# Side products of neighbouring heads and column tiles issued side by side, in a hybrid Mamba and attention layer pair

## The chip, the cores and the metric

The kernel runs on one core of one Trainium2 chip. The metric is the device time of one execution in microseconds (us); three runs of the kernel before gave 1612.24, 1612.61 and 1613.0 us, so the median is 1612.61 us. Every duration below comes from one profiled execution of the same kernel. Engines are called as the profile calls them: PE is the matrix engine, PEld its weight loads, DVE the vector engine, ACT the scalar engine, POOL the general-purpose engine, SP the engine whose queue issues most transfers.

## The reference

Two layers work on 256 tokens of width 2048, in 32-bit floats. The first is a Mamba2 layer with 64 heads in 8 groups, the second an attention layer with 32 heads of 128 channels whose logits carry a forget term. Cut to what the kernel has to compute:

```python
def mamba2_mixer(h, w_in, conv_w, conv_b, dt_bias, a_log, d_skip, norm_w, w_out):
    proj = h @ w_in                                  # 2048 -> 10304: z, x, B, C, dt
    xbc = silu(causal_depthwise_conv(xbc, conv_w, conv_b))
    y = ssd_chunked(xs, dt, a, bm, cm)               # (C B^T * decay) x, per head
    y = y + xs * d_skip
    y = gated_group_rmsnorm(y, z, norm_w)
    return y @ w_out                                 # 4096 -> 2048

def forgetting_attention_mixer(h, w_in, b_forget, w_out):
    proj = h @ w_in                                  # 2048 -> 16416: q, k, v, z, f
    cum = cumsum(log_sigmoid(f_logit + b_forget))
    for i in range(2):                               # blocks of 128 queries
        logits = q[i] @ k[:i + 1].T * scale + cum_q - cum_k, masked
        o[i] = softmax(logits) @ v[:i + 1]
    return (o * silu(z)) @ w_out                     # 4096 -> 2048

for i in range(2):
    x = x + mixer_i(rmsnorm(x, norm_w[i]))
return rmsnorm(x, final_norm_w)
```

The block of queries 0 to 127 sees only its own 128 keys, the block of queries 128 to 255 sees 256. Of each head's logits that makes a first block of 128x128 and a second of 128x256.

## The kernel before, in words

**Weight products.** Nearly all the work of PE is products of x or of an intermediate with weights that are streamed once from memory in tiles of 128x1024. A product of 32-bit floats is made of three products of a faster, shorter type (fp32r): ACT rounds a weight tile to its high form `wh` (`act_hi`, L102), DVE subtracts it from the tile and rounds the rest to the low form `wl` (`dve_lo`, L108), and the activations have high and low forms too. There are 7 buffers for raw tiles, 5 for `wh` and 4 for `wl`. Some of the products are arranged as Strassen-like sums, in which a tile is added to earlier ones as it is loaded (`sum_a`, `sum_b`, `sum_c`) and x is used in seven block combinations (`form`, `split_form`, L232).

**Side work.** Between the weight products stand small products and transposes that belong to no weight. In a Mamba group these are C times B transposed (`pcb`, L517), the transposes of the four 128-column tiles of x (`pxa`, L551), the product of the decay matrices with x for the head pair of each column tile (`py`, L598), the product with the state (`pof`) and the transposes of the gated result (`pyt`, L653). In a head of attention they are the transposes of q and k (`pqk`, L1017), the logits (`psc`, L1033), the transposes of the probabilities (`ppt`, L1069) and, at every second head, of z (`pz`, L1074), and the product with v (`po`, L1092 to L1095).

**What sets the order.** The program is a list of parts, each with the weight products of a half tile or of one sum. After each part `emit_due` issues the side work that has come due. `later(n, fn)` makes a step due n ordinary parts later; a part of a sum counts for half of one. For a head of attention the steps stand one part apart (`turn_qk`, `split_qk`, `logits`, `softmax`, `invert`, `turn`, `keep`, `values`, `close`), and the next head begins `gap` parts after the one before: 9 for most groups of four heads, 6 for the first and the last but one, 2 for the last. From this program a scheduler makes one fixed order of instructions for each engine, and PE, ACT, DVE, POOL and SP then run their own orders and wait for each other at semaphores.

**Accumulation banks.** In the Mamba layer 4 banks of PSUM hold weight products and 4 the side products, in the attention layer 5 and 3. A side step takes the next free bank of its pool.

**The layer boundary.** `to_layer2` (L780 to L788) adds the last output products to x, turns x (`pxt`, L795), rounds each of 16 tiles to a high and low form (`x`, L102 and L110), and makes the seven combinations of four pairs of tiles (`form`, then `ghx` on ACT and `glx` on DVE), which the first sums of the attention layer use. `stats2`, the forget gate (`forget`, `forget_sums`) and a round trip of its sums through memory (`cum_d`, `cB`) follow; each head's mask term `dd` (L1040) needs them.

Of the kernel before, what the change touches and what calls it, by code (L numbers as in the profile page):

```python
# [17 lines left out]
P = 128  # L18
# [5 lines left out]
G = 8  # L24
# [40 lines left out]
def hybrid_kernel(ctx: ExitStack, tc: tile.TileContext, a):  # L65
# [40 lines left out]
    def dve_lo(out, in_, hi, scale=None):  # L106
        if scale is None:
            nc.vector.tensor_tensor(out, in_, hi.bitcast(F32), op=ALU.subtract)  # L108
        else:
            nc.vector.scalar_tensor_tensor(  # L110
                out, in_, scale, hi.bitcast(F32), op0=ALU.mult, op1=ALU.subtract
            )

# [380 lines left out]
    def group_units(g):  # L494
# [13 lines left out]
        def post_c(ps):  # L508
            def done(o):
                st["C"] = o  # L510
                later(2, cb_pe)
                later(3, cb_dve)
            conv_silu(ps, 6 * g + 1, f"CT{g}", done)

        def cb_pe():
            st["pcb"] = pcb = bank(psa, "pcb")
            nc.tensor.matmul(pcb[:, 0:256], st["B"][:, 0:P], st["C"], start=True, stop=True)  # L517
            nc.tensor.matmul(pcb[:, 256:384], st["B"][:, P:S], st["C"][:, P:S],
                             start=True, stop=True)

        def cb_dve():
            st["cb"] = cb = lp.tile([P, 384], F32, tag="cb", name=f"cb{g}", bufs=2)
            nc.vector.tensor_tensor(cb, st["pcb"][:, :384], cst[:, C_MQ:C_MQ + 384],
                                    op=ALU.mult)
# [13 lines left out]
        def x_done(i, o):  # L538
            st[f"x{i}"] = o
            later(1 + wait, lambda: xa_pe(i))  # L540
            later(2 + wait, lambda: xa_dve(i))
            later(2 + wait + more, lambda: decay(i))
            later(4 + wait + more, lambda: y_pe(i))
            if i == 3:
                later(4 + wait + more, off_pe)
                later(5 + wait + more, off_dve)

        def xa_pe(i):
            st["pxa"] = pt = bank(psa, "pxa")
            for t in range(T2):  # L550
                nc.tensor.transpose(pt[:, t * P:t * P + P], st[f"x{i}"][:, t * P:t * P + P],  # L551
                                    ident)

        def xa_dve(i):
# [6 lines left out]
            c = slice(i * P, i * P + P)  # L561
            pt = st["pxa"]
            pt4 = pt[:, :S].rearrange("p (t h d) -> p t h d", t=T2, h=2)
# [10 lines left out]
        def decay(i):  # L574
            ee = lp.tile([P, 2, T2, P], F32, tag="ee", name="ee", bufs=3)
            for j in range(2):
                h = H0 + 2 * i + j
                for t in range(T2):
                    nc.scalar.activation(ee[:, j, t, :], st["acs"][i][:, j, t * P:t * P + P],
                                         AF.Relu, scale=-1.0, bias=beta[:, t, h:h + 1])  # L580
            nc.scalar.activation(ee, ee, AF.Exp, scale=-1.0)

            def mul():
                cb = st["cb"].rearrange("p (b l) -> p b l", b=3)
                nc.vector.tensor_tensor(
                    ee, ee, cb[:, 0:3:2, :].unsqueeze(1).to_broadcast([P, 2, T2, P]), op=ALU.mult)
                st[f"m{i}"] = ee
            later(1, mul)

# [24 lines left out]
        def post_z(pss, tiles):  # L614
# [12 lines left out]
            for i2 in range(2):  # L627
                later(4 + i2 + wait + more, lambda i2=i2: out_pe(i2))
                later(5 + i2 + wait + more, lambda i2=i2: out_split(i2))

# [144 lines left out]
    def to_layer2(n, t):  # L775


        if t == 1:
# [5 lines left out]
            if n == 3:  # L784
                later(2, stats2)
                for q in range(KS // 2):
                    later(2 + q, lambda q=q: split_form(
                        lay2["f"][q], True, lay2["forms"], 0, f"x{q}"))  # L788

    def x2_tiles(k0):  # L790
# [12 lines left out]
        for i in range(2):  # L803
# [7 lines left out]
            act_hi(xk[:, 0], pt[:, i * S:i * S + S], w)  # L811
            dve_lo(xk[:, 1], pt[:, i * S:i * S + S], xk[:, 0], w)

# [161 lines left out]
    def four_heads(hq, first=()):  # L975

        st = {}
        gap = {0: 6, G - 2: 6, G - 1: 2}.get(hq, 9)

# [3 lines left out]
        def vz_done(c):  # L983
# [9 lines left out]
            later(1, gate)  # L993
            steps = (turn_qk, split_qk, logits, softmax, invert, turn, keep, values, close)
            for i in range(4):
                for n, f in enumerate(steps, 1):
                    later(n + i * gap, lambda i=i, f=f: f(i))
# [23 lines left out]
        def split_qk(i):  # L1021
            h = fp[0].tile([P, 512], F32R, tag="qkh", name=f"qkh{hq}_{i}")
            l = fp[0].tile([P, 512], F32R, tag="qkl", name=f"qkl{hq}_{i}")
            act_hi(h, st["pqk"])
            dve_lo(l, st["pqk"], h)
            st["qkhl"] = (h, l)

        def logits(i):
            qkh, qkl = st["qkhl"]
            st["ps"] = ps = bank(psa, "psc")  # L1030
            for t, c, n in BLOCKS:
                for j, (q, k) in enumerate(((qkl, qkh), (qkh, qkh), (qkh, qkl))):
                    nc.tensor.matmul(ps[:, c:c + n], q[:, t * P:t * P + P], k[:, S:S + n],  # L1033
                                     start=j == 0, stop=j == 2)
            h = 4 * hq + i
# [251 lines left out]
```

## Time and profile before

| | |
|---|---|
| median of three runs | 1612.61 us (1612.24 to 1613.0) |
| the profiled execution, own time | 1618.07 us |
| its span | 1616.3 us |
| mean granted PE clock | 0.997 |
| PE busy | 1591.6 us, 98% of the span, 7862 instructions |
| DVE busy | 1342.0 us, 83% |
| ACT busy | 1061.6 us, 66% |
| POOL busy | 163.8 us, 10% |
| transfers | 362.30 MB, 224 GB/s over the span |

The profiled execution is 5.46 us longer than the median run, and 1.77 us of its time lies outside the span. The span is cut from one recorded execution; a row of a timeline gives the start, the duration, the engine, the line, the result and its inputs with the tile's shape, and how many instructions of that kind follow each other (x4). In brackets stands how long the engine idled before it and who released it. Starts of successive rows on PE tell the pace, since matmuls overlap and the duration of one row reaches into the next.

### The profile page before, as it was taken

What the parts mean: (1) busy time and instruction counts of PE and PEld (TensorE: products, weight loads), DVE (VectorE), ACT (ScalarE), POOL (GpSimd) and SP (SyncE); (2) the same over time, 40 slices, a digit from 0 to 9 for tenths busy, and PEclk for the clock granted to TensorE, in tenths of its full rate; (3) what the DMA queues carried; (4) which work ended last, traced back from release to release, by engine and by line L of the source; (5) the groups of instructions that cost most, each with busy time, mean ns of one, the idle gap of its engine ahead of it and who ended that gap; (6) DMA issues with size and microseconds to landing.
All of it is one profiled execution on the core that took longest, in us unless ns stands there. A gap on an engine that the chain in (4) does not pass through costs nothing. (4 is left out here: it accounts for less than half of the span.)

```text
span 1616.3 us, 22668 instructions
## 1 busy us (share of the span) xinstructions
PE 1591.6 (98%) x7862; PEld 1333.1 (82%) x7862; DVE 1342.0 (83%) x2006; ACT 1061.6 (66%) x1594; POOL 163.8 (10%) x214
## 2 busy tenths in 40 slices
PE   8999999999999999999999999999999999999997
PEld 6888888888888888778888888888888888888886
DVE  6888989798979897887888887888888887887886
ACT  7677777676767665755666665666665666676663
POOL 0000111011101110011100110010100101001000
PEclk9999999999999999999999999999999999999999
DMA  9665789778977897578887887897886987888843
GB/s 352 213 202 191 199 251 230 251 193 251 235 253 189 249 227 229 170 180 240 255 244 243 209 233 230 235 244 209 220 252 194 251 243 188 239 244 241 229 159 101
DMA packets 100964, 362.30 MB, mean 224 GB/s; under 512 B 11601, under 2 KB 12241, under 8 KB 100849
## 3 DMA queue, kind: packets, MB, share of 16 engines
q1 hardware_dynamic: 75888, 271.61, 48.4%
q0 software_dynamic: 24960, 89.24, 29.3%
q8 instruction: 62, 1.02, 0.2%
q14 instruction: 54, 0.43, 0.1%
HBM read 358.60 MB, written 2.20 MB: 223 GB/s over the span
## 5 line engine op out<-in xcount | busy, mean ns | idle before, releaser
L102 ACT ACTIVATE wh<-raw 128x1024 fp32r<-128x1024 f32 (+1 forms) x373 | 393.2, 1056 | 228.5 <-PE psa L288 73.8
L108 DVE TENSOR_TENSOR wl<-raw,wh 128x1024 fp32r<-128x1024 f32 (+1 forms) x373 | 451.5, 1216 | 82.4 <-issue 37.2
L102 ACT ACTIVATE wh<-sum_a 128x1024 fp32r<-128x1024 f32 x176 | 185.9, 1058 | 138.2 <-PE psy L924 32.6
L108 DVE TENSOR_TENSOR wl<-sum_a,wh 128x1024 fp32r<-128x1024 f32 x176 | 214.4, 1221 | 67.1 <-PE psu L924 36.6
L209 PE MATMUL pst<-x,wh 128*128 128x512 f32 x736 | 189.9, 398 | 0.1
L209 PEld LDWEIGHTS pst<-x,wh 128*128 128x128 f32 x736 | 134.0, 189 | 25.8 <-issue 0.5
L288 PE MATMUL psa<-wh,x 128*128 128x512 f32 x512 | 132.1, 399 | 0.0
L102 ACT ACTIVATE wh<-sum_b 128x1024 fp32r<-128x1024 f32 x88 | 93.2, 1060 | 55.1 <-PE psx L913 35.3
L108 DVE TENSOR_TENSOR wl<-sum_b,wh 128x1024 fp32r<-128x1024 f32 x88 | 106.7, 1219 | 9.8 <-issue 5.0
L288 PEld LDWEIGHTS psa<-wh,x 128*128 128x128 f32 x512 | 94.5, 188 | 21.6 <-issue 3.3
L213 PEld LDWEIGHTS pst<-x,wl 128*128 128x128 f32 x736 | 101.1, 192 | 7.5
L213 PE MATMUL pst<-x,wl 128*128 128x256 f32 x736 | 103.4, 284 | 0.0
L924 PE MATMUL psz<-wh,x 128*128 128x512 f32 x256 | 101.0, 394 | 0.0
L157 POOL DMA_DIRECT2D sum_a<-in_wf_s x64 | 55.3, 864 | 449.6 <-DVE wl L108 332.5
L924 PE MATMUL psv<-wh,x 128*128 128x512 f32 x256 | 100.6, 393 | 0.0
L924 PE MATMUL psy<-wh,x 128*128 128x512 f32 x256 | 99.8, 390 | 0.0
L924 PE MATMUL psu<-wh,x 128*128 128x512 f32 x256 | 99.7, 390 | 0.0
L690 DVE TENSOR_TENSOR xs<-psa,xs 128x512 f32<-128x512 f32 (+1 forms) x81 | 51.8, 678 | 26.1 <-PE psa L288 26.1
L288 PE MATMUL psa<-wh,ghf 128*128 128x512 f32 (+1 forms) x260 | 71.3, 394 | 0.0
L288 PE MATMUL psa<-wl,x 128*128 128x512 f32 x256 | 69.4, 391 | 1.2 <-DVE wl L108 1.2
L288 PE MATMUL psa<-wl,ghf 128*128 128x512 f32 (+1 forms) x260 | 69.4, 387 | 0.0
L288 PE MATMUL psa<-wh,glf 128*128 128x512 f32 (+1 forms) x260 | 69.3, 386 | 0.0
(356 smaller groups left out, 3312.7 us busy)
## 6 DMA issues: line engine op xcount, KB each, us to landing
raw<-in_wf_p SPq DMA_DIRECT2D x128, 512.0 KB, 4.9
raw<-in_wm_t SPq DMA_DIRECT2D x90, 512.0 KB, 4.8
raw<-in_wm_z SPq DMA_DIRECT2D x64, 512.0 KB, 5.4
sum_a<-in_wf_s POOLq DMA_DIRECT2D x64, 512.0 KB, 7.8
raw<-in_wf_o SPq DMA_DIRECT2D x64, 512.0 KB, 4.8
sum_a<-in_wm_s POOLq DMA_DIRECT2D x36, 512.0 KB, 5.9
sum_a<-in_wf_s SPq DMA_DIRECT2D x32, 512.0 KB, 6.8
sum_c<-in_wf_s SPq DMA_DIRECT2D x32, 512.0 KB, 5.3
```

What stands on the lines that cost most here:

```text
L102: nc.scalar.activation(out, in_, AF.Copy)
L108: nc.vector.tensor_tensor(out, in_, hi.bitcast(F32), op=ALU.subtract)
L157: nc.gpsimd.dma_start(u["sums"][name], src, accum_op=ALU.add)
L209: nc.tensor.matmul(ps, wh[:, k8 * P:k8 * P + P], ktile(v, k).rearrange("p i s -> p (i s)"), start=k == 0, stop=False)
L213: nc.tensor.matmul(ps[:, S:], wl[:, k8 * P:k8 * P + P], ktile(v, k)[:, 0], start=False, stop=k == KT - 1)
L288: nc.tensor.matmul(held[t][:, a:b], act(2 * n + k2, t)[i % 2], w[:, c], start=n == k2 == i == 0, stop=n == n_h - 1 and k2 == 1 and i == 2)
L690: nc.vector.tensor_tensor(c, pss[t][:, a:b], c, op=ALU.add)
L924: nc.tensor.matmul(ps[name], token(lay2["x"], k, t)[i % 2], w[:, k2 * 512:k2 * 512 + 512], start=first[t] and i == k2 == 0, stop=2 * n + k ...
```

## The change

Four things are done.

1. **Mamba groups 1 to 7.** `pcb` and the transposes of column tiles 0 and 1 (`pxa`) come due together, after the second column tile; the transposes of tile 2 come due with `py` of head pair 0, those of tile 3 with `py` of pair 1, and `py` of pairs 2 and 3 together. Each `pxa` has a bank name of its own in the program's state. The multiplication of pair 0's decay matrix with C B^T follows C B^T's copy directly. In all groups both halves of the transposes `pyt` come due in one place, and the two `out_split` come one part later.
2. **Heads of attention.** `gap` is 8 where it was 9, and the steps from `turn` on are placed so that `turn` of one head comes due with `turn_qk` of the next, `keep` with its `split_qk`, `values` with its `logits`. For the last group (gap 2) the steps stay where they were.
3. **The first logits block.** It was three fp32r products like the second block. It is one product of 32-bit floats, from a copy `qkr` (128x256) of the first q and k blocks that ACT makes from the same bank; `qkh` and `qkl` shrink from 512 to 384 columns.
4. **The layer boundary.** The combinations of x (`split_form`) are issued on DVE behind the low part of x's tile 11 (`tc.issue_after`).

```diff
--- before.py
+++ after.py
@@ -105,11 +105,9 @@
     def dve_lo(out, in_, hi, scale=None):
...
+            return nc.vector.tensor_tensor(out, in_, hi.bitcast(F32), op=ALU.subtract)
+        return nc.vector.scalar_tensor_tensor(
+            out, in_, scale, hi.bitcast(F32), op0=ALU.mult, op1=ALU.subtract)
@@ -508,17 +506,18 @@
         def post_c(ps):
             def done(o):
                 st["C"] = o
-                later(2, cb_pe)
-                later(3, cb_dve)
+                if g == 0:
+                    later(2, cb_pe)
+                    later(3, cb_dve)
             conv_silu(ps, 6 * g + 1, f"CT{g}", done)
 
-        def cb_pe():
+        def cb_pe(_=None):
             st["pcb"] = pcb = bank(psa, "pcb")
             nc.tensor.matmul(pcb[:, 0:256], st["B"][:, 0:P], st["C"], start=True, stop=True)
             nc.tensor.matmul(pcb[:, 256:384], st["B"][:, P:S], st["C"][:, P:S],
                              start=True, stop=True)
 
-        def cb_dve():
+        def cb_dve(_=None):
             st["cb"] = cb = lp.tile([P, 384], F32, tag="cb", name=f"cb{g}", bufs=2)
             nc.vector.tensor_tensor(cb, st["pcb"][:, :384], cst[:, C_MQ:C_MQ + 384],
                                     op=ALU.mult)
@@ -537,16 +536,27 @@
 
         def x_done(i, o):
             st[f"x{i}"] = o
-            later(1 + wait, lambda: xa_pe(i))
-            later(2 + wait, lambda: xa_dve(i))
+            if g == 0:
+                later(1 + wait, lambda: xa_pe(i))
+                later(2 + wait, lambda: xa_dve(i))
+            elif i > 0:
+                later(1, lambda: [f(n) for f, n in (
+                    ((cb_pe, None), (xa_pe, 0), (xa_pe, 1)) if i == 1 else
+                    ((xa_pe, i), (y_pe, i - 2)))])
+                later(2, lambda: [f(n) for f, n in (
+                    ((cb_dve, None), (lambda _: st["mul"](), None), (xa_dve, 0), (xa_dve, 1))
+                    if i == 1 else ((xa_dve, i),))])
             later(2 + wait + more, lambda: decay(i))
-            later(4 + wait + more, lambda: y_pe(i))
+            if g == 0:
+                later(4 + wait + more, lambda: y_pe(i))
             if i == 3:
+                if g > 0:
+                    later(4, lambda: [y_pe(2), y_pe(3)])
                 later(4 + wait + more, off_pe)
                 later(5 + wait + more, off_dve)
 
         def xa_pe(i):
-            st["pxa"] = pt = bank(psa, "pxa")
+            st[f"pxa{i}"] = pt = bank(psa, "pxa")
             for t in range(T2):
                 nc.tensor.transpose(pt[:, t * P:t * P + P], st[f"x{i}"][:, t * P:t * P + P],
                                     ident)
@@ -559,7 +569,7 @@
                 st["xd"] = xd[:, :T2 * 512].rearrange("p (t c) -> p t c", t=T2)
                 st["xg"] = lp.tile([P, 512], F32, tag="xg", name=f"xg{g}")
             c = slice(i * P, i * P + P)
-            pt = st["pxa"]
+            pt = st[f"pxa{i}"]
             pt4 = pt[:, :S].rearrange("p (t h d) -> p t h d", t=T2, h=2)
             d = dts[:, :, H0 + 2 * i:H0 + 2 * i + 2].unsqueeze(3).to_broadcast([P, T2, 2, HD])
             nc.vector.tensor_tensor(
@@ -585,7 +595,10 @@
                 nc.vector.tensor_tensor(
                     ee, ee, cb[:, 0:3:2, :].unsqueeze(1).to_broadcast([P, 2, T2, P]), op=ALU.mult)
                 st[f"m{i}"] = ee
-            later(1, mul)
+            if g > 0 and i == 0:
+                st["mul"] = mul
+            else:
+                later(1, mul)
 
         def y_pe(i):
             if i == 0:
@@ -625,8 +638,8 @@
                 later(1 + t + wait + more, lambda t=t: gate(t))
             later(3 + wait + more, norm)
             for i2 in range(2):
-                later(4 + i2 + wait + more, lambda i2=i2: out_pe(i2))
-                later(5 + i2 + wait + more, lambda i2=i2: out_split(i2))
+                later(5 + wait + more, lambda i2=i2: out_pe(i2))
+                later(6 + i2 + wait + more, lambda i2=i2: out_split(i2))
 
         def gate(t):
             xa, py, zs = st["xa"][:, t, :], st["py"][t], st["z"][:, t, :]
@@ -784,8 +797,7 @@
             if n == 3:
                 later(2, stats2)
                 for q in range(KS // 2):
-                    later(2 + q, lambda q=q: split_form(
-                        lay2["f"][q], True, lay2["forms"], 0, f"x{q}"))
+                    later(2 + q, lambda q=q: form_x(q))
 
     def x2_tiles(k0):
         x = lay2["x"]
@@ -809,7 +821,13 @@
                     pt[:, i * S:i * S + S].rearrange("p (t s) -> p t s", t=T2), AF.Copy, scale=w)
             xk = ktile(x, k)
             act_hi(xk[:, 0], pt[:, i * S:i * S + S], w)
-            dve_lo(xk[:, 1], pt[:, i * S:i * S + S], xk[:, 0], w)
+            lo = dve_lo(xk[:, 1], pt[:, i * S:i * S + S], xk[:, 0], w)
+            if k == 11:
+                lay2["behind"] = lo
+
+    def form_x(q):
+        with tc.issue_after(lay2["behind"].ins):
+            split_form(lay2["f"][q], True, lay2["forms"], 0, f"x{q}")
 
     def stats2():
         sq = small.tile([P, 2], F32, tag="ssq", name="ssqb")
@@ -975,7 +993,7 @@
     def four_heads(hq, first=()):
 
         st = {}
-        gap = {0: 6, G - 2: 6, G - 1: 2}.get(hq, 9)
+        gap = {0: 6, G - 2: 6, G - 1: 2}.get(hq, 8)
 
         def qk_done(c):
             st["qk"] = c
@@ -991,9 +1009,11 @@
             st["v"], st["z"] = (c[:, 1, :512], vh, vl), c[:, :, 512:]
             load_cum(0)
             later(1, gate)
-            steps = (turn_qk, split_qk, logits, softmax, invert, turn, keep, values, close)
+
+            last = max(1 + gap, 6)
             for i in range(4):
-                for n, f in enumerate(steps, 1):
+                for n, f in ((1, turn_qk), (2, split_qk), (3, logits), (4, softmax), (5, invert),
+                             (last, turn), (last + 1, keep), (last + 2, values), (last + 3, close)):
                     later(n + i * gap, lambda i=i, f=f: f(i))
 
         def gate():
@@ -1019,19 +1039,20 @@
                 load_cum(1)
 
         def split_qk(i):
-            h = fp[0].tile([P, 512], F32R, tag="qkh", name=f"qkh{hq}_{i}")
-            l = fp[0].tile([P, 512], F32R, tag="qkl", name=f"qkl{hq}_{i}")
-            act_hi(h, st["pqk"])
-            dve_lo(l, st["pqk"], h)
-            st["qkhl"] = (h, l)
+            h = fp[0].tile([P, 384], F32R, tag="qkh", name=f"qkh{hq}_{i}")
+            l = fp[0].tile([P, 384], F32R, tag="qkl", name=f"qkl{hq}_{i}")
+            r = fp[0].tile([P, 2, P], F32, tag="qkr", name=f"qkr{hq}_{i}")
+            act_hi(h, st["pqk"][:, P:])
+            dve_lo(l, st["pqk"][:, P:], h)
+            nc.scalar.copy(r, st["pqk"].rearrange("p (w t s) -> p w t s", w=2, t=2)[:, :, 0])
+            st["qkhl"] = (h, l, r)
 
         def logits(i):
-            qkh, qkl = st["qkhl"]
+            h, l, r = st["qkhl"]
             st["ps"] = ps = bank(psa, "psc")
-            for t, c, n in BLOCKS:
-                for j, (q, k) in enumerate(((qkl, qkh), (qkh, qkh), (qkh, qkl))):
-                    nc.tensor.matmul(ps[:, c:c + n], q[:, t * P:t * P + P], k[:, S:S + n],
-                                     start=j == 0, stop=j == 2)
+            nc.tensor.matmul(ps[:, :P], r[:, 0], r[:, 1], start=True, stop=True)
+            for j, (q, k) in enumerate(((l, h), (h, h), (h, l))):
+                nc.tensor.matmul(ps[:, P:P + S], q[:, :P], k[:, P:], start=j == 0, stop=j == 2)
             h = 4 * hq + i
             st["dd"] = dd = fp[0].tile([P, 384], F32, tag="dd", name="dd")
             cb = st[f"c{i // 2}"][:, i % 2, :]
```

What this makes of the engines' orders is seen at three places. The first is PE in Mamba group 4, at the products of C and B and the transposes of the column tiles `xT_0` to `xT_2`; weight products that stand between are left out. Before:

```order
L517 MATMUL pcb<-CT_3246,BT_3179 128x256
L518 MATMUL pcb<-CT_3246,BT_3179 128x128
...
L551 MATMUL pxa<-cst,xT_0_3324 128x128 x2
...
L551 MATMUL pxa<-cst,xT_1_3392 128x128 x2
...
L598 MATMUL py_3533<-xd_3465,ee 128x64
L598 MATMUL py_3534<-xd_3465,ee 128x64
...
L551 MATMUL pxa<-cst,xT_2_3459 128x128 x2
```

With the change:

```order
L516 MATMUL pcb<-CT_3246,BT_3179 128x256
L517 MATMUL pcb<-CT_3246,BT_3179 128x128
L561 MATMUL pxa<-cst,xT_0_3313 128x128 x2
...
L561 MATMUL pxa<-cst,xT_1_3392 128x128 x2
...
L561 MATMUL pxa<-cst,xT_2_3451 128x128 x2
L611 MATMUL py_3590<-xd_3531,ee 128x64
L611 MATMUL py_3591<-xd_3531,ee 128x64
```

The transposes of `xT_0` have moved back to stand behind `pcb`, and `py` of pair 0 has moved back behind the transposes of `xT_2`. The five places of side work shown before have become three.

The second place is PE in the attention layer, at the second head of a group (`qk_10717` before, `qk_10709` with the change, is that group's q and k). Before:

```order
L1069 MATMUL ppt<-cst,dd 128x128 x3
L1074 MATMUL pz<-cst,vz_11124 128x128 x4
...
L1092 MATMUL po<-ph,vl_11482 128x256
...
L1017 MATMUL pqk<-cst,qk_10717 128x128 x4
```

With the change:

```order
L1090 MATMUL ppt<-cst,dd 128x128 x3
L1095 MATMUL pz<-cst,vz_11115 128x128 x4
L1037 MATMUL pqk<-cst,qk_10709 128x128 x4
...
L1113 MATMUL po<-ph,vl_11482 128x256
L1114 MATMUL po<-ph,vh_11481 128x256
L1115 MATMUL po<-pl,vh_11481 128x256
L1116 MATMUL po<-p_11740,vz_11115 128x128
L1053 MATMUL psc<-qkr_1_11748 128x128
L1055 MATMUL psc<-qkh_1_11746,qkl_1_11747 128x256
```

The transposes of the next head's q and k now follow those of this head's probabilities with nothing between, and the next head's logits follow this head's product with v.

The third place is ACT at head 0 of the first group of heads, where `qkh_0_7642` (and with the change `qkr_0_7644`) is made. Before:

```order
L102 ACTIVATE qkh_0_7642<-pqk 128x512
L102 ACTIVATE wh<-sum_b 128x1024
L900 ACTIVATE qk_7627<-psx,rstQ_6855 128x512
L102 ACTIVATE wh<-raw 128x1024 x2
L102 ACTIVATE wh<-sum_a 128x1024 x2
```

With the change:

```order
L102 ACTIVATE qkh_0_7642<-pqk 128x384
L102 ACTIVATE wh<-sum_b 128x1024
L918 ACTIVATE qk_7627<-psx,rstQ_6855 128x512
L102 ACTIVATE wh<-raw 128x1024 x2
L1047 COPY qkr_0_7644<-pqk 128x256
L102 ACTIVATE wh<-sum_a 128x1024 x2
```

The high form is smaller and stands where it stood; the new copy comes four instructions after it, behind the rounding of two raw weight tiles.

More of the change, by code (lines that the diff above doesn't have):

```diff
@@ L107, in dve_lo @@
         if scale is None:
[L108 to L112, printed above, removed]
+            return nc.vector.tensor_tensor(out, in_, hi.bitcast(F32), op=ALU.subtract)
+        return nc.vector.scalar_tensor_tensor(
+            out, in_, scale, hi.bitcast(F32), op0=ALU.mult, op1=ALU.subtract)
     def rsqrt(out, in_, mul, add):
```

## The prediction

> **What bounds the kernel now.** I read the profile's page first, then PE's waits, then PE's timeline at the places that the change touches, and last ACT and DVE ahead of those places. The page and the list of PE's waits (line waited at, what for, total us, times, longest) say:
>
> ```profile
> PE 1591.6 (98%) x7862; PEld 1333.1 (82%) x7862; DVE 1342.0 (83%) x2006; ACT 1061.6 (66%) x1594; POOL 163.8 (10%) x214
> PE ppt L1069 <- ACT dd L1062: 2.0, 3, 0.9
> PE pxt L795 <- DVE x L110: 1.8, 1, 1.8
> PE pyt L653 <- ACT xa L646: 1.2, 4, 0.4
> PE po L1095 <- ACT p L1082: 1.0, 2, 0.8
> ...
> PE psx L913 <- ACT wh L102: 0.2, 1, 0.2
> PE psx L913 <- DVE wl L108: 0.2, 1, 0.2
> ```
>
> PE works 98% of the span; no other engine is above 83%. So the time is the sum of what PE issues and of a few places where it waits. A term counts only if it takes work off PE, makes PE wait less or makes it wait anew. The weight products are the same 6724 instructions in both orders; all that follows is about the side work between them. A block of four 512-column weight products starts 0.91 us after the one before it; I call this the pace and charge a side group with what it puts between such blocks beyond the pace.
>
> **First logits block, −3.2 us.** A head's logits on PE before, and the product with v, which already has the make-up that the logits will have (three fp32r products of 256 columns, and a product of 32-bit floats of 128 columns, which shows as two instructions):
>
> ```profile
> 993.78 1.07 PE L288 MATMUL psa<-wl,ghf 128*128 128x512 f32 x4
> 994.69 0.22 PE L1033 MATMUL psc<-qkh,qkl 128*128 128x128 f32 x1
> ...
> 994.97 0.33 PE L1033 MATMUL psc<-qkh,qkl 128*128 128x256 f32 x1
> ...
> 995.37 1.09 PE L288 MATMUL psa<-wh,ghf 128*128 128x512 f32 x4
> 996.30 1.07 PE L288 MATMUL psa<-wh,glf 128*128 128x512 f32 x4
> 1009.82 0.28 PE L1092 MATMUL po<-ph,vl 128*128 128x256 f32 x1
> ...
> 1010.17 0.39 PE L1095 MATMUL po<-p,vz 128*128 128x128 f32 x2
> 1010.32 0.71 PE L913 MATMUL psx<-wh,ghx 128*128 128x512 f32 x2
> 1010.86 0.63 PE L913 MATMUL psx<-wh,glx 128*128 128x512 f32 x2
> ```
>
> The six products take 994.69 to 995.37, 0.68 us, and the four behind them 0.93 instead of 0.91: 0.70 us. The product with v takes 0.50 (1009.82 to 1010.32) and leaves the next two weight products 0.54 instead of 0.46 (half of 0.91): 0.58, rounded up to 0.60. The difference is 0.10 us for each of 32 heads, 3.2 us; with 0.58 it is 3.8, and with a fp32 product dearer by 0.02 it is 2.6.
>
> The Trainium skill speaks against this term: TensorE: Matmul & The Clock Gate, section "Back-to-back issue gap", gives about 81 ns for each matmul of 128 columns in a sustained stream, by which three cost 243 ns, hardly more than one 32-bit product, and the term would shrink to about −0.6 by an estimate from that page. Here six products cost 0.70 us, 0.117 each, more than the page's figure, and the trace decides; no run so far shows the one product alone.
>
> **Fewer side groups, −1.5 us.** Counted in the two orders of PE, the places where weight products are broken by side work fall from 212 to 144. What a break costs besides its own products is what is seen above: 0.02 us behind the logits, up to 0.08 behind the product with v (part of which is its 32-bit product). At 0.03 the 68 breaks make −2.0; about 12 places lose the order in which `py` and transposes overlapped, of the size of one break each, +0.5. Bounds 0 and −3.4 (0.05 a break).
>
> **PE's waits at the transposes of the gated result, −2.7 us.** One of the four places:
>
> ```profile
> 230.16 0.62 PE L726 MATMUL psx<-wl,ghm 128*128 128x512 f32 x2
> 231.03 0.33 PE L653 MATMUL pyt<-cst,xa 128*128 128x128 f32 x1 [0.25 <-ACT xa L646]
> 231.11 0.48 PE L209 MATMUL pst<-x,wh 128*128 128x512 f32 x1
> 231.64 0.55 PE L653 MATMUL pyt<-cst,xa 128*128 128x128 f32 x3
> 231.95 1.41 PE L209 MATMUL pst<-x,wh 128*128 128x512 f32 x5
> ```
>
> From 230.16 to 231.95 are 1.79 us; three weight products at 0.227 (0.91 by four) and four transposes at 0.11 (three take 231.64 to 231.95) are 1.12. So the place loses 0.67 although 0.25 is recorded as idle; four such make 2.7. The change issues both halves of these transposes one part later, about 4.2 us of weight products behind where the normalised rows were just late by half a microsecond. The wait goes altogether, and nothing needs the transposes sooner: the sums that use them are a pair of groups away, and `out_split` is later by a part as well. If PE instead arrives early by what it gains elsewhere, it is early by less than 1 us of 4.2. Bounds −1.2 (the recorded idle alone) and −2.8.
>
> **PE's waits at a head's probabilities, −3.3, and at the product with v, −1.3 us.** The worst of three and the longer of two, the second with ACT's rows ahead of it:
>
> ```profile
> 796.52 0.39 PE L924 MATMUL psy<-wl,x 128*128 128x512 f32 x1
> 797.61 0.84 PE L1069 MATMUL ppt<-cst,dd 128*128 128x128 f32 x3 [0.70 <-ACT dd L1062]
> 798.28 0.60 PE L1074 MATMUL pz<-cst,vz 128*128 128x128 f32 x4
> 798.64 0.71 PE L913 MATMUL psu<-wh,ghx 128*128 128x512 f32 x2
> 1402.93 1.06 ACT L102 ACTIVATE wh<-raw 128x1024 fp32r<-128x1024 f32 x1 [3.18 <-DMA raw<-in_wf_p]
> 1404.20 0.49 PE L1095 MATMUL po<-p,vz 128*128 128x128 f32 x2 [0.80 <-ACT p L1082]
> ```
>
> From 796.52 to 798.64 are 2.12 us for one weight product (0.23) and seven transposes (0.77): 1.12 lost. The three places by the same working lose 1.1, 1.4 and 0.8. With the change `turn` stands where the next head's transposes of q and k are due, two to three parts later; putting the new order of PE on the clock of the weight products before, the probabilities are ready 2 us or more ahead of it in every head but one of the last group (0.7), mostly 5 to 13. The product with v loses 1.0 as recorded and 0.15 at each restart; it too moves later, and the copy that it waits for is ready 2 us ahead or more. Bounds for the two together −3.0 (recorded idle) and −4.6. What is late next is not on these chains, since the weight products before a step are unchanged and only more of them lie between a step and the next.
>
> **The transposes of x's column tiles, −0.3 us.** At three places they start behind the pace, as here:
>
> ```profile
> 171.51 0.39 PE L209 MATMUL pst<-x,wh 128*128 128x512 f32 x1
> 171.94 0.44 PE L551 MATMUL pxa<-cst,xT 128*128 128x128 f32 x2
> ```
>
> 171.51 and 0.23 make 171.74, so 0.2 is lost. With tiles 0 and 3 issued later this goes (−0.6); the new neighbours, `pcb` and `py` of pair 0, have their inputs several us ahead in the mapping, but one late input now holds a longer group. I take half; bounds −0.6 and +1.
>
> **The layer boundary, −1.0 us.** PE's longest wait behind the start of the kernel, and DVE's rows before it:
>
> ```profile
> 681.79 1.07 PE L288 MATMUL psa<-wl,ghm 128*128 128x512 f32 x4
> 684.61 0.41 PE L795 MATMUL pxt<-cst,xs 128*128 128x128 f32 x2 [1.75 <-DVE x L110]
> 682.00 1.08 DVE L108 TENSOR_TENSOR glx<-form,ghx 128x896 fp32r<-128x896 f32 x1
> 682.99 0.68 DVE L690 TENSOR_TENSOR xs<-psa,xs 128x512 f32<-128x512 f32 x1
> 683.60 0.86 DVE L110 SCALAR_TENSOR_TENSOR x<-pxt,vec,x 128x256 fp32r<-128x256 f32 x2
> ```
>
> PE's last product starts its four at 681.79 and ends them at 682.70; the transposes need the sums `xs` and a free bank, which the low parts of x give back. DVE is busy with `glx` from 682.00 to 683.0, and the change issues `glx` behind the low part of tile 11, so the sums start up to 1.0 sooner, but the wait goes on for two sums and the low parts between them, 2 times 0.68 and 0.86, or 2.2 us of DVE work. I take −0.7 of the 1.8. PE's two short waits at `psx` for `wh` and `wl`, soon after the boundary (0.2 each, 0.35 each with the restart of 0.15 seen at other waits) I count as gone, −0.7. Against that the forms, the forget gate's sums and with them the mask terms come some us later, behind a round trip through memory; +0.4. Bounds −2.0 and +3 (the whole lead of PE lost at the first head's mask).
>
> **The new copy, +3.4 us.** ACT makes `qkr` from the bank of `pqk`, which DVE reads too. What it costs and where it stands:
>
> ```profile
> L267 ACT COPY rest<-pst 128x256 f32<-128x256 f32 x48 | 17.2, 358 | 1.6 <-DVE cu L268 1.3 <-DVE vt L268 0.3
> L1082 ACT COPY p<-ppt 128x128 f32<-128x128 f32 x32 | 8.1, 253 | 5.3 <-DVE pl L108 5.3
> 994.03 1.06 ACT L102 ACTIVATE wh<-raw 128x1024 fp32r<-128x1024 f32 x1 [1.66 <-PE psa L288]
> 991.49 0.68 DVE L108 TENSOR_TENSOR qkl<-pqk,qkh 128x512 fp32r<-128x512 f32 x1
> 789.74 1.06 ACT L102 ACTIVATE wh<-raw 128x1024 fp32r<-128x1024 f32 x1 [3.58 <-PE psz L913]
> 787.87 0.22 PE L1033 MATMUL psc<-qkh,qkl 128*128 128x128 f32 x1
> ```
>
> A copy of this shape takes 0.36 us, and like `p` before it, it waits for DVE's read of the same bank (5.3 us of ACT's idle time, 32 times). The Trainium skill's page PSUM — Partial Sum Buffer, section "PSUM bank collisions raise a hardware error", says that two engines must not be in one bank at once; the rows of `p` agree. At a usual head this is hidden: at 992.1 `qkl` is done, the copy would run to 992.5 in ACT's gap before 994.03, and PE starts the logits at 994.69. On the mapped clock it is ready 1.1 us ahead or more everywhere but at two heads: 0.4 at the first head of the last group but one, and 3.2 too late at the first head of all. There the copy stands behind two roundings of raw tiles, and the second was held until 789.74 by its load; it ends at 790.7, the copy at 791.1, and PE wants it at 787.87. With the restart that is +3.4. Bounds 0 (the tile lands earlier, or the place is as late for another reason) and +4.5. The smaller `qkh` and `qkl` give ACT and DVE some 0.15 us a head, which is off PE's path.
>
> **The sum** is −3.2 −1.5 −2.7 −3.3 −1.3 −0.3 −1.0 +3.4 = −9.9 us. The profiled execution of 1618.07 us becomes 1608.2. It is 5.46 above the median, and nothing in the terms belongs to that difference, so for the median I say 1612.61 − 9.9 = 1602.7 us. With all bounds at their good ends it would be near 1595, with the bad ends of the larger ones together near 1610.
>
> **Rivals.**
>
> *The copy comes late in many heads.* ACT runs in a fixed order; where a raw tile is late, what stands behind its rounding is late, as at 789.74 and 1402.93 (3.58 and 3.18 us). Now every head's logits hang on a copy behind one or two such roundings. From 0.3 us a head on (9.9 by 31) it eats the gain. If half the heads wait 1 us, +16: 1602.7 + 16 = 1618.7 us, slower than before. For it: heads with a lead of only 0.4 to 1.3 us. Against it: PE's list of waits shows only two places at `p`, which stands behind roundings in the same way in 32 heads.
>
> *The waits move along with the work.* PE gains nothing at the transposes and products with v because their inputs come later too: only the logits, the breaks and the boundary's terms are left, −3.2 −1.5 −1.0, with half of the new wait +1.7: 1608.6 us. For it: ACT and DVE follow PE, since they wait for its free buffers. Against it: the steps' inputs keep their distance from the step before, and the consumer alone moves.
>
> *The short products hold PE less than their share.* Of the logits' 0.70 us the three products of 128 columns take 0.28 by their starts (994.69 to 994.97), since the first of them slips in behind the weight product. One 32-bit product takes 0.15 (1010.17 to 1010.32) and the 0.08 that the next two products lose, 0.23. Then a head gains 0.05, all of them 1.6 instead of 3.2 us: 1604.3 us. Against it: by the sums of whole groups, 0.70 and 0.60, the gain is 0.10. The section of the Trainium skill named above points further in this direction, to some 1605 us by the estimate given there.
>
> **How the numbers follow.** The sum has 0.74; the late copies 0.08; the waits that move along 0.14; the cheap short products 0.04. About 0.2% (3.2 us) can be told from no change here, so faster means below 1609.4 and slower above 1615.8. The sum lies below it nearly whole (0.72), the waits that move along by six parts in ten, the last whole: 0.84 faster. Slower is the late copies' 0.07; 0.09 is left for the same. The range goes from 1596.5 (the waits in full, the first head's copy in time) to 1609.5, which takes in the second and third rival.
>
> **What would show it.** Right: PE's list of waits without `pyt` and `ppt`, one new row of about 3 us for the logits waiting for ACT's copy near 788 us, the logits at 0.58 to 0.60 instead of 0.70 with the same pace around them, and `pxt` at about 1 us. Wrong: many waits at the logits for the copy, or waits at `py`, `pxa` or the mask chain in place of the old ones; weight products behind the pace without a recorded wait would say that the sum of PE's work was priced wrongly.

## The result and the profile after

The changed kernel takes 1604.47 us (median of six runs, 1602.40 to 1607.25) where the kernel before, timed beside it, takes 1613.06 (1612.24 to 1614.32): a ratio of 0.9948 with a 95% interval of 0.9935 to 0.9960, or 8.4 us less by that ratio (8.6 between the two medians). Two later sets of runs of the same kernel gave 0.9937 (0.9925 to 0.9950) and 0.9941 (0.9925 to 0.9956). Predicted were 1602.7 us and −9.9.

The page of the changed kernel, and its list of PE's waits (line waited at, what for, total us, times, longest):

```profile
PE 1580.8 (99%) x7830; PEld 1329.9 (83%) x7830; DVE 1335.0 (83%) x2006; ACT 1062.6 (66%) x1626; POOL 163.9 (10%) x214
```

```profile
PE pst L250 <- ACT wh L102: 5.9, 3, 4.6
PE psc L1053 <- ACT qkr L1047: 3.0, 2, 1.8
PE psa L286 <- DVE wl L108: 1.2, 1, 1.2
PE pk L860 <- DVE lf L854: 1.2, 1, 1.2
PE psr L314 <- DVE dg L313: 0.7, 1, 0.7
PE pxt L807 <- DVE xs L703: 0.7, 1, 0.7
PE psx L931 <- DVE wl L108: 0.4, 1, 0.4
PE psv L931 <- DVE wl L108: 0.3, 1, 0.3
```

PE is still the engine that sets the time, and it now works 99% of the span. The rows for the transposes of the gated result (`pyt`), the probabilities (`ppt`) and the product with v (`po`) are gone. `pxt` fell from 1.8 to 0.7. Besides one of 0.3 us at `psv`, two rows are new: the logits wait for ACT's copy (`psc` for `qkr`, two places), and the forget gate's sums (`pk`) for DVE. The two places of the first, and between them a logits block that does not wait, on PE:

```profile
784.20 0.49 PE L1053 MATMUL psc<-qkr 128*128 128x128 f32 x2 [1.18 <-ACT qkr L1047]
...
986.16 1.07 PE L286 MATMUL psa<-wl,ghf 128*128 128x512 f32 x4
987.07 0.38 PE L1053 MATMUL psc<-qkr 128*128 128x128 f32 x2
...
987.64 1.08 PE L286 MATMUL psa<-wh,ghf 128*128 128x512 f32 x4
988.56 1.07 PE L286 MATMUL psa<-wh,glf 128*128 128x512 f32 x4
...
1438.02 0.49 PE L1053 MATMUL psc<-qkr 128*128 128x128 f32 x2 [1.78 <-ACT qkr L1047]
```

That block takes 987.07 to 987.64, 0.57 us, and the four products behind it 0.92: with what these take beyond their pace of 0.91, 0.58 us, where it was 0.70. ACT ahead of the second of the late places:

```profile
1430.19 0.47 ACT L102 ACTIVATE qkh<-pqk 128x384 fp32r<-128x384 f32 x1
...
1432.08 1.06 ACT L102 ACTIVATE wh<-raw 128x1024 fp32r<-128x1024 f32 x1
1436.65 1.06 ACT L102 ACTIVATE wh<-raw 128x1024 fp32r<-128x1024 f32 x1 [3.52 <-DMA raw<-in_wf_p]
1437.62 0.35 ACT L1047 COPY qkr<-pqk 128x256 f32<-128x256 f32 x1
```

The high form was ready at 1430.7. The copy stands behind two roundings of raw tiles, and ACT stood still 3.52 us for the second tile; the copy follows it at 1437.62, and PE starts the logits at 1438.02. At 784 us the same four instructions stand in the same order, with 2.88 us of waiting for the tile.

### The profile page after: what moved, and what is told of

It is laid out like the page before. It is cut to its first block, busy times and chain, and to the rows that moved or that the text cites. A ratio compares the mean times of both kernels' runs of the same rounds, so it can differ in the third digit from the quotient of the medians.

```text
span 1604.0 us, 22659 instructions
## 1 busy us (share of the span) xinstructions
PE 1580.8 (99%) x7830; PEld 1329.9 (83%) x7830; DVE 1335.0 (83%) x2006; ACT 1062.6 (66%) x1626; POOL 163.9 (10%) x214
## 5 line engine op out<-in xcount | busy, mean ns | idle before, releaser
L207 PE MATMUL pst<-x,wh 128*128 128x512 f32 x736 | 185.4, 394 | 0.1
```

The source lines that it names most:

```text
L207: nc.tensor.matmul(ps, wh[:, k8 * P:k8 * P + P], ktile(v, k).rearrange("p i s -> p (i s)"), start=k == 0, stop=False)
```

## The experiments

**The four parts alone.** Each part was put into the kernel before by itself. First the logits:

```diff
+            nc.scalar.copy(r, st["pqk"].rearrange("p (w t s) -> p w t s", w=2, t=2)[:, :, 0])
...
+            nc.tensor.matmul(ps[:, :P], r[:, 0], r[:, 1], start=True, stop=True)
+            for j, (q, k) in enumerate(((l, h), (h, h), (h, l))):
+                nc.tensor.matmul(ps[:, P:P + S], q[:, :P], k[:, P:], start=j == 0, stop=j == 2)
```

> Only the logits' first block is made as one 32-bit product from the new copy; order and gaps as before. Theory of the sum: the logits fall from about 0.69 to 0.58 us a head (-3.5 us for 32), and PE waits newly for the copy only where it stands behind a late raw tile, at the first head of the first group (about 3 us) and perhaps at one head near the end: near -0.5 to -2 us against the kernel before, its waits for probabilities, transposes of the gated result and the product with v still there. Rival, the copy is late in many heads: 5 or more rows of waits at the logits, 0 or slower. Rival, short products nearly free: logits at 0.64 us, gain under 2 us even without waits.

Measured: 1614.34 us against 1613.72, a ratio of 1.0001 (0.9992 to 1.0009): no gain, where −0.5 to −2 us were expected. Its list of PE's waits has one row for the copy, one place and not the five of the rival:

```profile
PE psc L1033 <- ACT qkr L1027: 1.4, 1, 1.4
```

Then the Mamba groups:

```diff
+            elif i > 0:
+                later(1, lambda: [f(n) for f, n in (
+                    ((cb_pe, None), (xa_pe, 0), (xa_pe, 1)) if i == 1 else
+                    ((xa_pe, i), (y_pe, i - 2)))])
...
-                later(4 + i2 + wait + more, lambda i2=i2: out_pe(i2))
+                later(5 + wait + more, lambda i2=i2: out_pe(i2))
```

> Only the Mamba groups' side products are grouped anew. Theory of the sum: the waits at the transposes of the gated result go (about 2.7 us with restarts) and those at the transposes of x's column tiles (0.6), and 26 fewer breaks of the weight products at 0.03 make 0.8: -4 us. Rival, breaks are free: -3.3 us, and a row of groups shows the grouped products as dear as the single ones. Rival, the waits move along with the work: -1 us and the waits show again one part later.

Measured: 1610.64 us, 0.9979 (0.9969 to 0.9988), −3.4 us (−1.9 to −5.0), which does not part the sum of −4 from the −3.3 of breaks that are free. The `pyt` row is gone from its waits, and no row of a Mamba step took its place. Then the heads' steps:

```diff
-        gap = {0: 6, G - 2: 6, G - 1: 2}.get(hq, 9)
+        gap = {0: 6, G - 2: 6, G - 1: 2}.get(hq, 8)
...
+            last = max(1 + gap, 6)
```

> Only the gaps and the placing of the heads' steps change; logits of six products as before. Theory of the sum: the waits at the probabilities (3.3) and at the product with v (1.3) go, 42 fewer breaks at 0.03 make 1.3: -5.9 us. Rival, breaks are free: -4.6 us. Rival, the waits move along: -1 to -2 us with waits at the same lines as before.

Measured: 1610.77 us, 0.9977 (0.9969 to 0.9986), −3.7 us (−2.3 to −5.0), less than the −5.9 expected. Neither `ppt` nor `po` is among its waits. Last the layer boundary:

```diff
+    def form_x(q):
+        with tc.issue_after(lay2["behind"].ins):
+            split_form(lay2["f"][q], True, lay2["forms"], 0, f"x{q}")
```

> Only x's combinations are queued behind the low part of tile 11. Theory of the sum: the wait at the turning of x falls from 1.8 to about 0.7 us as in the changed kernel, and the forget gate's sums arrive late by about 1.2 us in exchange: 0 to -1 us. Rival, a loss: the first sums or the mask of the first head wait for the later forms, +1 to +3 us.

Measured: 1612.23 us, 0.9991 (0.9983 to 1.0000), −1.5 us. Its list of PE's waits has the boundary's row reduced, and two rows behind it that the kernel before has not:

```profile
PE psv L916 <- DVE wl L108: 1.9, 2, 1.2
...
PE pk L845 <- DVE lf L839: 1.0, 1, 1.0
...
PE pxt L792 <- DVE xs L688: 0.7, 1, 0.7
```

The four differences add up: 0 − 3.4 − 3.7 − 1.5 = −8.6, and the whole change gave −8.4. Each of these has an interval of 1.4 to 2 us to either side, so that the sum fits to 0.2 is partly chance; no interaction shows beyond that scatter. It remains to be seen why the logits, which are 0.12 us shorter a head, gave nothing.

**The copy directly behind the high form.** In the changed kernel and in the one with the logits alone, the copy was put ahead of DVE's low form:

```diff
             act_hi(h, st["pqk"][:, P:])
+            nc.scalar.copy(r, st["pqk"].rearrange("p (w t s) -> p w t s", w=2, t=2)[:, :, 0])
             dve_lo(l, st["pqk"][:, P:], h)
-            nc.scalar.copy(r, st["pqk"].rearrange("p (w t s) -> p w t s", w=2, t=2)[:, :, 0])
```

> The kernel before with only the logits' first block as one 32-bit product, and the copy made directly behind the high form. The same block with the later copy gave 1.0001 of the time before. If waits for the copy ate its gain, this one is 3 to 4 us faster than the kernel before (32 heads by 0.11 us). If the 32-bit product saves nothing in the sum, it stays within 1 us of the kernel before.

Measured: 1611.20 us against 1613.66, 0.9983 (0.9974 to 0.9992), −2.7 us (−1.3 to −4.2), where the same product with the late copy gave nothing. The place of the copy alone is thus worth about 2.9 us in this kernel, by two sets of runs that are each uncertain by 1.4. In this profile no wait at `psc` is left, and the five instructions of the logits step in 0.58 us in each of the 32 heads, where the six took 0.69 in each head of both profiles of the kernel before.

The profile of the late copy shows one such wait of 1.4 us, in an execution of 1611.86 us that was itself 2.5 below its kernel's median. What the other executions lost is not seen in a trace. Their mean granted clock was 0.996 or less in five of the twelve with the late copy (1615.6 us on average, the other seven 1612.8), and in none of the eleven with the early one. That stops for the copy bring this on is not shown: no profile has a drop of the clock behind one, and three of the eleven runs of the Mamba groups alone have so low a mean too.

> The changed kernel with one line moved: ACT makes the 32-bit copy of q and k directly behind the high form, ahead of DVE's low form. Theory of the sum: the two waits of the logits for the copy (3.3 us with restarts in the profile of the changed kernel, at 784 and 1438 us) go, DVE's low form comes 0.36 us later, which its lead of 1.5 us or more covers: about 3 us faster than the changed kernel, -11.5 us against the kernel before. Rival, the waits belong to the late raw tiles and only move to the low form, which stands behind the same work: no better than the changed kernel, with waits at the logits for the low form.

> The changed kernel with the copy directly behind the high form, a second time. Theory: no wait of the logits, 1.5 to 3 us (0.1 to 0.2%) below the changed kernel timed beside it. Rival: the earlier difference (0.9934 against 0.9948 and 0.9937) was scatter and the two come out alike within 0.05%.

Measured: 1603.46 us, 0.9934 (0.9922 to 0.9947), and the second time 1603.24, 0.9928 (0.9917 to 0.9940), with the changed kernel beside it at 1605.55. Between the medians that is 2.3 us side by side; between sets of runs the ratios differ by 0.5 to 2.3 us. The intervals of the two kernels overlap, so by time alone the move is not clear of the scatter; that the waits are gone is seen in the profiles. At head 0, in the profile of the first of these kernels, ACT and then PE:

```profile
775.97 0.47 ACT L102 ACTIVATE qkh<-pqk 128x384 fp32r<-128x384 f32 x1
776.34 0.36 ACT L1046 COPY qkr<-pqk 128x256 f32<-128x256 f32 x1
...
781.30 1.06 ACT L102 ACTIVATE wh<-raw 128x1024 fp32r<-128x1024 f32 x1 [2.11 <-DMA raw<-in_wf_p]
```

```profile
781.82 0.38 PE L1053 MATMUL psc<-qkr 128*128 128x128 f32 x2
```

ACT still stands 2.11 us for the raw tile, but the copy is done 5 us before PE wants it; no wait at `psc` is left in either profile. The low form, issued behind the copy, makes none either: DVE ends it at 780.32, 1.6 us before the product that reads it.

**Steps one part apart.** The heads' later steps were kept from meeting the next head's:

```diff
-            last = max(1 + gap, 6)
+            last = max(1 + gap, 6) + (gap == 8)
```

> The changed kernel with the turning of probabilities, keep, product with v and close one part later in groups of gap 8, so that they no longer meet the next head's steps: 30 more breaks of the weight products (174 instead of 144), all else alike. Theory of the sum, 0.03 us a break: about 1 us slower than the changed kernel, and the trace shows it as slow steps of the weight products behind side work, with no new waits. Rival, breaks are free: no difference in the sum of PE's steps. Rival, pairing matters by more than the break (0.1 us each): 3 us slower.

Measured: 1605.00 us, 0.9947 (0.9933 to 0.9960): by time it cannot be told from the changed kernel (0.9937 to 0.9948). So the steps of PE's rows, from start to start with the recorded waits left out, were added up between the 3400th and the 6300th weight product, about 770 to 1490 us: for side work the whole step, for a weight product what it takes above 0.227 us (512 columns) or 0.120 (256). That makes 59.6 us in the changed kernel (59.7 and 59.4 in its other two profiles) and 60.9 here: 1.2 to 1.5 us for 30 breaks, 0.04 to 0.05 each. Apart, the side work's own steps are shorter (52.4 us against 54.7), and the weight products lose more (8.5 against 4.9), most of it in the first two behind a break. A second pair says the same with less: the boundary alone, with the heads' old order, and the heads alone, neither with a wait in this stretch, make 64.3 and 62.9, which is 1.4 us for 41 breaks, 0.03 each.

**Second looks.** Both kernels were profiled again, to see which waits belong to the order and which to one execution.

> The kernel before, unchanged, for a second profile. The prediction charged 4.6 us to waits at the probabilities and at the product with v, read from one execution that was 5.5 us above the median. Theory: these waits hang on when a raw tile lands and differ from one execution to the next; a second execution shows 0 to 2.5 us of them while the waits at the transposes of the gated result stay 4 rows and 1.2 us. Rival: they belong to the order and show again at 2.0 and 1.0 us.

```profile
PE pxt L795 <- DVE x L110: 1.7, 1, 1.7
...
PE pyt L653 <- ACT xa L646: 1.2, 4, 0.4
PE psz L924 <- DVE wl L108: 1.0, 1, 1.0
PE ppt L1069 <- ACT dd L1062: 0.9, 1, 0.9
```

This execution took 1614.39 us. `pyt` and `pxt` are as they were; `ppt` has one place instead of three, and `po` none. In the other profiles with the old order these rows stand in the lists of the logits alone, first with the late and then with the early copy, and of the Mamba groups alone:

```profile
PE po L1096 <- ACT p L1083: 0.8, 1, 0.8
...
PE po L1096 <- ACT p L1083: 1.7, 2, 1.1
PE ppt L1070 <- ACT dd L1063: 0.7, 1, 0.7
...
PE ppt L1084 <- ACT dd L1077: 0.4, 1, 0.4
```

Over the six profiles that have the heads' old order (the two of the kernel before, the logits alone in both forms, the Mamba groups alone, the boundary alone) the recorded waits at `ppt` and `po` together are 3.0, 0.9, 0.8, 2.4, 0.4 and 0 us, 1.3 on average. In the eight profiles with the heads' new order they are 0.

> The changed kernel, unchanged, for a second profile and further times. Theory: the two waits of the logits for the copy (head 0 of the first group and of the last but one) come back with other sizes, between 0.5 and 3 us each, as the raw tile lands; no waits at the probabilities or the product with v; ratio 0.993 to 0.996. Rival: the waits belong to the order and come back with the same 1.2 and 1.8 us.

```profile
PE pk L860 <- DVE lf L854: 2.2, 1, 2.2
PE psc L1053 <- ACT qkr L1047: 1.5, 2, 1.1
```

> The changed kernel, unchanged, beside the one with the copy moved, on one chip. Theory: waits of the logits for the copy at the same two places, 0.5 to 3 us each; ratio to the kernel before 0.993 to 0.996.

The logits waited 1.5 us in all in the one (at 787 and 1439 us) and 1.3 us in the other (one place), after 3.0 in the first profile. The places are those of the order, the lengths those of the execution; two of the four, 0.4 us and none at all, are below the half microsecond expected.

**The mask terms behind.** On top of the moved copy, each head's mask term was queued on DVE behind its low form, and the forget gate's sums were to come later:

```diff
+            with tc.issue_after(st["lo"].ins):
+                for t, c, n in BLOCKS:
...
-        later(5, lambda: forget_sums(lf))
+        later(6, lambda: behind(lambda: forget_sums(lf)))
```

> The changed kernel with the copy directly behind the high form, each head's mask term queued on DVE behind that head's low form, and the forget gate's sums one part later and queued on PE behind the weight products ahead of them. Theory: the wait for the forget gate's sums (1.3 us with restart) goes and DVE no longer stands for 3.7 us at the first mask term, so nothing new waits: 1 to 1.5 us faster than the kernel with the copy moved alone (0.9934), near 0.9926. Rival: the later mask terms make the probabilities late, or the wait moves to the round trip through memory: no better than 0.9934, with waits at the probabilities.

Measured: 1601.50 us, 0.9916 (0.9902 to 0.9930), the lowest of all. But the wait that it was to remove is still there, since the sums kept their place in PE's order:

```profile
722.54 0.62 PE L864 MATMUL pk<-cst,lf 128*32 128x256 f32 x2 [1.26 <-DVE lf L854]
```

Ahead of these sums stand 3203 weight products, as in the changed kernel. Only the mask term moved, and DVE's stand in front of it is gone, which in the changed kernel was this:

```profile
733.91 0.35 DVE L1061 SCALAR_TENSOR_TENSOR dd<-cB,cum_q,cst 128x128 f32<-128x128 f32 x1 [3.69 <-DMA cB<-cum_d]
```

The changed kernel beside it came to 0.9937, and the moved copy alone, in other sets, to 0.9934 and 0.9928. Its interval does not part it from those of the moved copy; whether the mask's move adds anything stays open.

## Why the prediction was nearly right

The direction held, and the time lies 1.8 us above the forecast, inside the range. That it lies so near is partly luck: the waits of the heads were priced some 2.6 us too high, the logits and the breaks together 1 to 2 us too low. By its own steps:

- **First logits block, −3.2.** By the rows 0.70 became 0.58, so −0.12 a head and −3.8 us for 32, the end that the prediction named for a product of 0.58. Timed alone with an early copy it gave −2.7 (−1.3 to −4.2). The time would leave room for the 1.6 us of the rival by which the short products hold PE less than their share; the rows of all 32 heads do not, so that rival is out. The Trainium skill's figure in TensorE: Matmul & The Clock Gate, section "Back-to-back issue gap", of about 81 ns for a matmul of 128 columns, would by the prediction's estimate have let the block fall by 0.02 us or so; it fell by 0.12, so the trace and not the page priced it.
- **Fewer breaks, −1.5.** Near: the profiles give 0.03 to 0.05 us a break where 0.03 was taken; by that the 68 breaks make −2.3 to −3.4 where the sum had −2.0. The +0.5 for lost overlaps was not measured.
- **Transposes of the gated result, −2.7, and of x's tiles, −0.3.** Right for the first: the row is in every profile of the old order at 1.2 us in four places and in none of the new, and the Mamba groups alone gave −3.4, their breaks included. The waits did not move along. What x's tiles gave was not measured by itself.
- **Probabilities and product with v, −4.6.** This is the step that failed, and with it the sentence that nothing in the terms belongs to the 5.46 us by which the profiled execution lay above the median. The mechanism held, since the new order shows none of these waits. But the long ones hang on when raw tiles land (ACT stood 1.88 us for one ahead of the wait at 836 us and 3.18 ahead of the one at 1404), and that one execution had 3.0 us of them recorded where the six profiles average 1.3. By that ratio the term is near −2 (an estimate), not −4.6. All the heads' steps together, breaks included, gave −3.7 (−2.3 to −5.0), where the prediction's terms make −5.5.
- **The layer boundary, −1.0.** The sum was near (−1.5 alone, 0 to −2.7), its pieces were not. The wait at `pxt` fell by 1.1 instead of 0.7. The short waits behind it stayed instead of going. The forget gate's sums came late on PE itself, by 1.0 to 1.3 us in five of the eight profiles and 1.7 to 2.2 in three, where +0.4 was said. And a piece was missing, the clock (below).
- **The copy, +3.4.** The place and the cause were right: head 0 of the first group, the copy behind a rounding whose raw tile is late. The size there was 1.2 us (1.3 with the restart) instead of 3.4, since the tile had landed earlier against PE's position (its rounding began 0.2 us before PE wanted the logits, in the kernel before 1.9 us behind); but the head to which the prediction gave a lead of 0.4 us, first of the last group but one, waited 1.8. Together 3.0, and 1.5 and 1.3 in the second and third profile. The sum came out near by two misses that cancel. The moved copy took back about 2, near the edge of the scatter.

Of the rivals, the copy was late at two heads and not in many, in the kernel as changed. In the kernel with the logits alone the late copy cost the part's whole gain, 2.7 us, of which one wait of 1.4 is seen; where the rest went stays open.

## What to carry to other kernels

A wait that hangs on a transfer has a place, which the order gives, and a length, which the single execution gives: price it from several profiles, and where the profiled run lies above the median, ask first which of its waits the median does not have. A new instruction on an engine that runs in a fixed order costs most by what stands ahead of it: a copy of 0.36 us behind two roundings of loaded tiles cost about 2.9 us in one pair of kernels and about 2 in another, and one line higher nothing that shows. Time the parts alone: four measured parts that add up to the whole show that one of them gave nothing, which the whole could not show.

## What the runs showed of the hardware

The stop at the boundary cost more than its idle time. In four of the six profiles in which PE stood about 1.75 us at `pxt`, the granted clock then fell to about half for some 3.4 us; the same three microseconds in the first profile of the kernel before, in its second, and in the changed kernel (start and end, width, busy time of each engine, then the granted clock):

```profile
686.00:689.00 3.00, 3.00 (x13) 2.63 (x12) 2.36 (x14) 1.16 (x2) 0.86 (x1) 0.57 0.52 165
```

```profile
686.00:689.00 3.00, 3.00 (x21) 2.74 (x21) 2.42 (x11) 2.03 (x3) 0.86 (x1) 1.00 0.57 168
```

```profile
686.00:689.00 3.00, 3.00 (x17) 2.56 (x16) 3.00 (x6) 2.32 (x5) 0.00 (x0) 1.00 0.41 138
```

Weight products of 512 columns then step at 0.427 us instead of 0.227 and those of 256 at 0.213 instead of 0.120; from the start of the transposes to the first weight product behind the boundary the first profile takes 5.54 us (684.61 to 690.14) and the second, at the full clock, 3.99 (684.06 to 688.05), so the drop cost about 1.5 us. After the stop of 0.7 us that is left with the change, none of the eight profiles with it shows this at the boundary. It came back elsewhere, behind the stop at `pk`, in two of those eight: in the second and third profile of the changed kernel, behind 2.2 and 1.2 us, the third reading:

```profile
724.00:727.00 3.00, 3.00 (x8) 2.31 (x7) 1.23 (x1) 1.52 (x4) 0.56 (x1) 0.50 1.02 418
```

In the second profile it lasted twice as long, from 723 to 730 us. The other six, with stops of 1.0 to 1.9 us, keep the full clock there, so the length of the stop alone does not decide. The new wait thus has that price too, now and then.

The Trainium skill, TensorE: Matmul & The Clock Gate, section "Why this matters for your kernels", advises against PE standing still for more than about 3 us between bursts; here 1.2 and 1.75 us were at times enough, so the runs and not the page's figure decide; that it happens in some executions only agrees with the free-running window of activity that the page describes in Part 1.
